# Own buffers for residual loads, spills issued by ScalarE, score banks for the cross output, and two activation sums moved beside cross attention, in a hybrid encoder step on one core

## The chip, the cores and the metric

The kernel runs on one core of a Trainium2 chip. A time is the device time of one execution in microseconds (us). The kernel before takes 1830.3 us, the median of 3 runs (1829.97 to 1832.38). One more execution was profiled; all rows below come from it. It took 1833.62 us, of which 1831.8 us lie between its first and its last instruction (the span).

The engines are named as in the profile: PE multiplies matrices, PEld loads its weights, DVE, ACT and POOL work elementwise, SP issues transfers (DMA). Each engine takes its instructions in order, so an instruction that waits holds back all that stand behind it on its engine. That holds for issues of transfers too: a transfer that is not yet allowed to start holds back the next ones of the same engine.

## The reference

One layer of a streaming encoder, on 1024 prompt frames and 32 sample frames of width 1024, in float32:

```python
z = rms_norm(x, g_mix) @ w_in            # q k v conv_h conv_B conv_C gate_a gate_b
a = window_attention(q, k, v) @ w_attn_out
bo = (cb * causal_conv3(cc * ch)) @ w_conv_out
x = x + (sigmoid(ga) * a + sigmoid(gb) * bo) @ w_mix_out
hc = rms_norm(x, g_cross)                # 4 heads x 64 against 256 memory tokens
x = x + softmax((hc @ w_cq) @ mem_k.T / 8) @ mem_v @ w_co
hm = rms_norm(x, g_mlp)
x = x + square(relu(hm @ w_up)) @ w_down # hidden width 4096
y = rms_norm(x, g_final)
```

It also returns new keys, values, convolution rows and memory keys and values.

## The kernel before

**Layout.** Activations lie transposed, features on the 128 partitions, frames along the free axis. The 1056 frames are cut into three chunks, 0, 1 and 2, of 384, 384 and 288 frames; 1024 features are eight blocks, numbered by f or k. Every float32 number is split in a high part (a rounded copy, made by ACT) and a low part (the rest, a subtraction on DVE), and a product is three matmuls: high by high, low by high, high by low (`gemm`, lines 166 to 168). A gemm over eight blocks is 24 matmuls.

**Weights.** A weight tile of 128x1024 is loaded by SP into `wr` (2 buffers), cast by ACT to `wh` (line 114, or 140 where the low part is fetched) and subtracted by DVE to `wl` (line 115), 3 buffers each. `next_w` keeps up to three weights prepared ahead of the gemm that uses them. Some weights are used for every chunk; for every second of them (`kept`) the low part is written to DRAM when it is first made (`wl_d`, line 145) and read back later (line 139).

**Stages.** After input projection, window attention, convolution and gates come, chunk by chunk, `trunk(c)` (eight items `do_conv_out`, eight items `do_mix`), and cross attention `cross_steps(c)`: statistics, two query products (`do_cq`), per head `scores`, `turn` (transpose of the softmax) and `values`, then two items `do_co` and statistics. `beside` interleaves them: one step of `cross_steps(c)` after each item of `trunk(c+1)`, so that PE has a gemm while DVE and ACT do the softmax. The steps of chunk 2 stand beside the first quarter of the MLP's up product, `up0(0)` and `up0(1)`. `normed_split` (lines 923 to 929) makes the MLP's input for chunks 0 and 1: DVE makes `ct`, SP writes it to DRAM as `xn_d`, ACT and DVE split it.

**Up product.** The other three quarters of the up product for chunks 0 and 1 use a 2x2 product with fewer multiplications. It needs sums of activation blocks: T2, N1, N3, N4 for each k of 0 to 3. `combine(k)` (lines 958 to 973) reads four blocks of `xn_d` into `lt` and makes all four sums and their parts; it runs beside the up products of chunk 2 (`do_up(j, 2)`). POOL also adds pairs of weights there (`s`, lines 992 to 995).

**Buffers.** Temporaries of all kinds share six buffers `ct` (`tmp`), the loads of `m1_d` in `do_conv_out` and of the input `x` in `do_mix` too. PE's results go to PSUM: three buffers `acc`, two banks for the scores `sc` (tag `s`), two `pt`, one `o`. `do_co` puts its four results per item into `acc`.

**Order.** Instructions are ordered per engine by a scheduler that works with a model of times when the program is built; `pin` keeps some in program order. The order is then fixed.

Of the kernel before, what the change touches and what calls it, by code (L numbers as in the profile page):

```python
# [10 lines left out]
F32 = mybir.dt.float32  # L11
F32R = mybir.dt.float32r
AF = mybir.ActivationFunctionType
ALU = mybir.AluOpType
# [4 lines left out]
P = 128  # L19
# [4 lines left out]
NF = 8  # L24
# [14 lines left out]
def hybrid_step(ctx: ExitStack, tc: tile.TileContext, io):  # L39
    nc = tc.nc  # L40
    act, dve, pool_e, pe, sp = nc.scalar, nc.vector, nc.gpsimd, nc.tensor, nc.sync
# [3 lines left out]
    def nm(s):  # L45
        uid[0] += 1
        return f"{s}_{uid[0]}"
# [14 lines left out]
    ps = ctx.enter_context(tc.tile_pool(name="ps", bufs=1, space=PSUM))  # L62
# [16 lines left out]
    xn_d = [dram.tile([P, NF, n], F32, name=f"xn_d{c}") for c, (_, n) in enumerate(CH[:2])]  # L79
# [4 lines left out]
    def pin(ins):  # L84
        return tc.keep_in_program_order(ins)

    def acc_tile(shape):
        return ps.tile(shape, F32, tag="acc", bufs=3, name=nm("acc"))

    def tmp(n, dt=F32):  # L90
        return tp.tile([P, n], dt, tag="ct", bufs=NCT, name=nm("ct"))
# [9 lines left out]
    plan, worder, kept = [], [], {}  # L101
# [29 lines left out]
    def issue_w():  # L131
        if not fetched:
            fetch_w()
        raw = fetched.pop(0)
        key = worder[wpos[0]]
        hi = wp.tile([P, 1024], F32R, tag="wh", name=nm("wh"))
        lo = wp.tile([P, 1024], F32R, tag="wl", name=nm("wl"))
        if kept.get(key) is not None:
            sp.dma_start(lo.bitcast(F32), kept[key])
            act.copy(hi, raw)  # L140
        else:
            split(hi, lo, raw)
            if key in kept:
                kept[key] = dram.tile([P, 1024], F32, name=nm("wl_d"))
                sp.dma_start(kept[key], lo.bitcast(F32))
        ready.append((worder[wpos[0]], (hi, lo)))
        wpos[0] += 1

# [494 lines left out]
    for i, h in enumerate(hosts):  # L643
# [9 lines left out]
        if h[0] == "Q":  # L653
            fn, key = do_Q(h[1], h[2], extras), qt(h[1], h[2])
        elif h[0] == "K":
            fn, key = do_K(h[1], extras), ("w_in", 8 + h[1])
        elif h[0] == "G":
            fn, key = do_gate(h[1], extras), ("w_in", 34 + h[1])
# [71 lines left out]
    def gain_split(x, g, c):  # L730
        hi, lo = yslot(c), yslot(c)
        scaled_split(hi, lo, x, g)
        return hi, lo

    def do_conv_out(c, f):
        def fn(w):
            n = CH[c][1]
            t1 = tmp(n)
            sp.dma_start(t1, m1_d[c][:, f])
            a = acc_tile([P, n])  # L740
            gemm(a, w, bcp[c])
            t = tmp(n)
            dve.tensor_mul(t, a, sg[c][f])  # L743
            (dve if f == NF - 1 else pool_e).tensor_tensor(t, t, t1, op=ALU.add)  # L744
            mg[c][f] = (mslot(n), mslot(n))
            split(*mg[c][f], t)

        return fn

    def do_mix(c, f):  # L750
        def fn(w):
            n = CH[c][1]
            xt = tmp(n)
            sp.dma_start(xt, io[f"x{c}"][:, f])
            a = acc_tile([P, n])
            gemm(a, w, mg[c])
            x = gate_slot(c, f)
            dve.tensor_add(x, a, xt)  # L758
            x1[c][f] = x
            xc[c][f] = gain_split(x, G_CROSS + f, c)  # L760
            square_acc(x, f, c, on_pool=f < NF - 1)

        return fn
# [30 lines left out]
    qc, co = {}, [[None, None] for _ in CH]  # L794
# [91 lines left out]
    def do_co(c, half):  # L886
        def fn(w):
            n = CH[c][1]
            wh, wl = w
            fs = range(4 * half, 4 * half + 4)  # L890
            for f in fs:
                a = acc_tile([P, n])
                for k in range(2):
                    s = slice(((f % 4) * 2 + k) * P, ((f % 4) * 2 + k) * P + P)
                    hi, lo = co[c][k]
                    pe.matmul(a, wh[:, s], hi, start=(k == 0), stop=False)
                    pe.matmul(a, wh[:, s], lo, start=False, stop=False)
                    pe.matmul(a, wl[:, s], hi, start=False, stop=(k == 1))
                x = x1[c][f]
                dve.tensor_add(x, a, x)  # L900
                if half == 0 and c == 2:
                    xm[c][f] = gain_split(x, G_MLP + f, c)
                square_acc(x, f, c)
            if half == 1 and c == 2:
                for f in fs:
                    xm[c][f] = gain_split(x1[c][f], G_MLP + f, c)

        return fn
# [11 lines left out]
    def lt(n=384):  # L920
        return L["pool"].tile([P, n], F32, tag="lt", bufs=6, name=nm("lt"))

    def normed_split(c, f):
        t = tmp(CH[c][1])
        pin(dve.scalar_tensor_tensor(t, x1[c][f], col(G_MLP + f), R[c], op0=ALU.mult, op1=ALU.mult))
        sp.dma_start(xn_d[c][:, f], t)
        hi, lo = xm[c][f] = (yslot(c), yslot(c))
        act.copy(hi, t)
        pin(dve.tensor_sub(lo, t, hi.bitcast(F32)))

    def hidden(c, j, h):
# [21 lines left out]
    def comb_slot(kind, k):  # L953
        if kind in ("N1", "N3"):
            return mslot(384)
        return L["pool"].tile([P, 384], F32R, tag="hx", bufs=8, name=nm("hx")) if k < 2 else yslot(1)

    def combine(k):
        b12, b22, b11, b21 = (lt() for _ in range(4))
        for t, c, f in ((b12, 1, k), (b22, 1, k + 4), (b11, 0, k), (b21, 0, k + 4)):  # L960
            sp.dma_start(t, xn_d[c][:, f])
        n3, n1, t2, n4 = b22, b12, b11, b21
        pin(dve.tensor_sub(n3, b12, b22))
        pin(dve.tensor_sub(n1, b11, b12))
        pin(dve.tensor_sub(t2, b11, n3))
        pin(pool_e.tensor_tensor(n4, b21, t2, op=ALU.subtract))
        for kind, x in (("T2", t2), ("N1", n1), ("N3", n3), ("N4", n4)):
            hi, lo = comb[kind, k] = (comb_slot(kind, k), comb_slot(kind, k))
            act.copy(hi, x)
            if kind[0] == "T" or kind == "N1":  # L970
                pin(dve.tensor_sub(lo, x, hi.bitcast(F32)))
            else:
                pin(pool_e.tensor_tensor(lo, x, hi.bitcast(F32), op=ALU.subtract))

# [174 lines left out]
    def beside(steps, fillers, late=()):  # L1151
        for i, filler in enumerate(fillers):
            item(*filler)
            for x in [x for at, x in late if at == i]:
                item(lambda x=x: x())
            if steps:
                kind, what = steps.pop(0)
                for x in what:
                    if kind == "items":
                        item(*x)  # L1160
                    else:
                        item(lambda x=x: x())
        return steps
# [9 lines left out]
    left = beside([], trunk(0))  # L1173
    left = beside(cross_steps(0), trunk(1))

    normed = lambda c, at: [(at + f, lambda f=f: normed_split(c, f)) for f in range(NF)]
    left = beside(left + cross_steps(1), trunk(2), normed(0, 6))
    left = beside(left + cross_steps(2), up0(0) + up0(1), normed(1, 0))
    assert not left
    for j in range(NF):  # L1180
        item(*do_up(j, 2))
# [223 lines left out]
```

## Time and profile before

| | us | note |
|---|---|---|
| median of 3 runs | 1830.3 | 1829.97 to 1832.38 |
| profiled execution | 1833.62 | |
| its span | 1831.8 | mean granted clock of PE 0.993 |
| PE busy | 1797.5 | 98% |
| DVE busy | 1045.2 | 57% |
| ACT busy | 720.3 | 39% |
| POOL busy | 356.4 | 19% |

The table gives busy time in the whole span. Trunk and cross attention lie at about 800 to 1165 us, the up products of chunk 2 with `combine` at about 1165 to 1210 us. In rows that show instructions, the columns are start, duration, engine, line, operation, result<-operands, and in brackets the idle time of the engine before it with the instruction that ended it. A row of stretches gives the stretch, its length, the busy time of PE, PEld, DVE, ACT and POOL with their instruction counts, the clock that PE was granted (1.00 is full), the share of DMA time, and GB/s. A row of waits gives the total, the number and the longest.

### The profile page before, as it was taken

How to read it: one execution, taken by the hardware profiler on the slowest of the kernel's cores; microseconds unless marked ns; L12 is line 12 of the kernel's file. 1: busy time of each engine (PE TensorE's matmuls, PEld its weight loads, DVE VectorE, ACT ScalarE, POOL GpSimd, SP SyncE). 2: the span in 40 equal slices, each digit the busy share in tenths (PEclk: the TensorE clock that was granted, in tenths of full speed). 3: DMA queues.
4: the chain of work that ended last, by engine and by line, in shares of the span. 5: the costliest groups of instructions: out<-in, count | busy, mean ns of one | idle time of the engine just before them, and what ended most of it. 6: DMA issues, size and time to landing. Idle time of an engine off the chain costs nothing.

```text
span 1831.8 us, 29560 instructions
## 1 busy us (share of the span) xinstructions
PE 1797.5 (98%) x11364; PEld 1780.0 (97%) x11364; DVE 1045.2 (57%) x2007; ACT 720.3 (39%) x1414; POOL 356.4 (19%) x381
## 2 busy tenths in 40 slices
PE   7999999999999999999999899999999999999997
PEld 7999999999999999999999899999999999999997
DVE  7766766757664222436575877766555664242255
ACT  7643535434354101324555655532222443030134
POOL 3211010211100000004333231564433000000023
PEclk9999999999999999999999999999999999999999
DMA  5411111112123124227656666833322664131144
GB/s 177 141 62 62 62 56 60 67 60 71 56 82 119 55 94 134 96 77 244 243 180 227 221 214 217 289 119 103 108 95 88 217 222 149 50 113 42 67 146 145
DMA packets 112205, 230.40 MB, mean 126 GB/s; under 512 B 13344, under 2 KB 74944, under 8 KB 111936
## 3 DMA queue, kind: packets, MB, share of 16 engines
q1 hardware_dynamic: 112064, 228.51, 37.1%
q8 instruction: 90, 1.47, 0.3%
q14 instruction: 51, 0.42, 0.1%
HBM read 181.98 MB, written 46.48 MB: 125 GB/s over the span
## 4 chain that ended last, share of the span: by engine, by line
PE 91%; DVE 3%; DMA 2%; POOL 1%; issue 1%; ACT 1%; SPq 0%; POOLq 0%; DVEq 0%; ACTq 0%
PE acc L166 23%; PE acc L167 23%; PE acc L168 23%; PE acc L1010 3%; PE acc L1012 3%; PE acc L1011 3%; PE pt L535 1%; PE pa L167 1%; PE pa L168 1%; PE pa L166 1%; DVE wl L115 1%; PE sc L510 1%; PE sc L509 1%; DMA ct<-in_x 1%; PE o L548 1%
## 5 line engine op out<-in xcount | busy, mean ns | idle before, releaser
L114 ACT CAST wh<-wr 128x1024 fp32r<-128x1024 f32 x200 | 210.0, 1050 | 486.9 <-PE acc L167 387.4
L166 PE MATMUL acc<-X,wh 128*128 128x384 f32 (+1 forms) x1200 | 390.5, 325 | 8.4 <-ACT wh L114 7.9
L167 PE MATMUL acc<-X,wh 128*128 128x384 f32 (+1 forms) x1200 | 387.8, 323 | 2.0 <-DVE X L241 1.9
L168 PE MATMUL acc<-X,wl 128*128 128x384 f32 (+1 forms) x1200 | 386.8, 322 | 0.3 <-DVE wl L115 0.3
L166 PE MATMUL acc<-Y,wh 128*128 128x384 f32 (+1 forms) x1008 | 326.5, 324 | 1.3 <-DVE ct L940 0.6
L168 PE MATMUL acc<-Y,wl 128*128 128x384 f32 (+1 forms) x1008 | 326.0, 323 | 0.0
L167 PE MATMUL acc<-Y,wh 128*128 128x384 f32 (+1 forms) x1008 | 325.7, 323 | 0.0
L115 DVE TENSOR_TENSOR wl<-wr,wh 128x1024 fp32r<-128x1024 f32 x200 | 267.4, 1337 | 72.9 <-ACT wh L114 72.2
L166 PEld LDWEIGHTS acc<-X,wh 128*128 128x128 f32 x1200 | 226.3, 189 | 9.1 <-ACT wh L114 7.9
L167 PEld LDWEIGHTS acc<-X,wh 128*128 128x128 f32 x1200 | 226.6, 189 | 3.5 <-DVE X L241 3.0
L168 PEld LDWEIGHTS acc<-X,wl 128*128 128x128 f32 x1200 | 226.2, 189 | 0.8 <-DVE wl L115 0.8
L166 PEld LDWEIGHTS acc<-Y,wh 128*128 128x128 f32 x1008 | 189.1, 188 | 2.3 <-DVE ct L940 0.8
L167 PEld LDWEIGHTS acc<-Y,wh 128*128 128x128 f32 x1008 | 189.2, 188 | 0.0
L168 PEld LDWEIGHTS acc<-Y,wl 128*128 128x128 f32 x1008 | 189.1, 188 | 0.0
L237 POOL TENSOR_TENSOR xacc<-xacc,ct 128x384 f32<-128x384 f32 (+1 forms) x62 | 78.3, 1265 | 356.8 <-ACT ct L235 352.0
L166 PE MATMUL acc<-M,wh 128*128 128x384 f32 (+1 forms) x320 | 104.9, 329 | 0.3 <-DVE Ga L758 0.3
L167 PE MATMUL acc<-M,wh 128*128 128x384 f32 (+1 forms) x320 | 104.3, 327 | 0.0
L168 PE MATMUL acc<-M,wl 128*128 128x384 f32 (+1 forms) x320 | 104.3, 326 | 0.0
L114 ACT CAST PTh<-pt 128x512 fp32r<-128x512 f32 (+3 forms) x94 | 46.3, 516 | 129.6 <-PE pt L535 122.4
L744 POOL TENSOR_TENSOR ct<-ct,ct 128x384 f32<-128x384 f32 (+1 forms) x21 | 25.5, 1214 | 364.7 <-DVE ct L743 329.5
L1121 DVE TENSOR_TENSOR Gb<-acc,Gb 128x384 f32<-128x384 f32 (+1 forms) x60 | 31.4, 523 | 110.7 <-PE acc L168 110.7
L166 PE MATMUL acc<-H,wh 128*128 128x288 f32 (+1 forms) x256 | 80.7, 315 | 0.0
(283 smaller groups left out, 3483.7 us busy)
## 6 DMA issues: line engine op xcount, KB each, us to landing
wr<-in_w_down SPq DMA_DIRECT2D x56, 512.0 KB, 3.3
wr<-in_w_in SPq DMA_DIRECT2D x50, 512.0 KB, 3.2
wr<-in_w_up SPq DMA_DIRECT2D x48, 512.0 KB, 3.8
wl<-wl_d SPq DMA_DIRECT2D x28, 512.0 KB, 4.5
wr<-in_w_conv_out SPq DMA_DIRECT2D x24, 512.0 KB, 4.3
wr<-in_w_mix SPq DMA_DIRECT2D x24, 512.0 KB, 4.0
ct<-hid_d SPq DMA_DIRECT2D x64, 192.0 KB, 3.6
hid_d<-lt SPq DMA_DIRECT2D x48, 192.0 KB, 1.8
```

The lines of the kernel that those rows point to most:

```text
L114: act.copy(hi, src)
L115: dve.tensor_sub(lo, src, hi.bitcast(F32))
L166: pe.matmul(out, wh[:, a], hi, start=(k == 0), stop=False)
L167: pe.matmul(out, wh[:, a], lo, start=False, stop=False)
L168: pe.matmul(out, wl[:, a], hi, start=False, stop=(k == len(acts) - 1))
L237: pool_e.tensor_tensor(acc, acc, sq, op=ALU.add)
L509: pe.matmul(sc[:, h, j * w : j * w + w], q[h], a, start=True, stop=False)
L744: (dve if f == NF - 1 else pool_e).tensor_tensor(t, t, t1, op=ALU.add)
L1010: pe.matmul(acc, wh[:, a], hi, start=(start and k == 0), stop=False, skip_group_check=True)
L1011: pe.matmul(acc, wh[:, a], lo, start=False, stop=False, skip_group_check=True)
L1012: pe.matmul(acc, wl[:, a], hi, start=False, stop=(k == 3), skip_group_check=True)
L1121: dve.tensor_add(x, a, x)
```

## The change

Five edits. (1) `ld(n)`: four buffers of its own, in the pool of cross attention, for the loads in `do_conv_out` and `do_mix`. (2) The 14 writes of `wl_d` and the 16 writes of `xn_d` are issued by ACT in place of SP. (3) `do_co` puts the first two of its four results into the two banks of the scores. (4) `combine_n(k)` makes N3 and N1 from three loads into `ld`, after items 4, 6, 8 and 9 of the up product beside cross attention of chunk 2; `combine(k)` keeps T2 and N4, and makes N3 once more without splitting it, since T2 needs it. (5) `normed_split` takes the blocks in the order 0, 4, 1, 5, 2, 6, 3, 7.

```diff
-                sp.dma_start(kept[key], lo.bitcast(F32))
+                act.dma_start(kept[key], lo.bitcast(F32))
...
+    def ld(n):
+        return cr.tile([P, n], F32, tag="ld", bufs=4, name=nm("ld"))
...
-            t1 = tmp(n)
+            t1 = ld(n)
             sp.dma_start(t1, m1_d[c][:, f])
...
-            xt = tmp(n)
+            xt = ld(n)
             sp.dma_start(xt, io[f"x{c}"][:, f])
...
+            two = ps.tile([P, 2, 512], F32, tag="s", name=nm("co"))
             for f in fs:
-                a = acc_tile([P, n])
+                a = two[:, f % 4, :n] if f % 4 < 2 else acc_tile([P, n])
...
-        sp.dma_start(xn_d[c][:, f], t)
         hi, lo = xm[c][f] = (yslot(c), yslot(c))
         act.copy(hi, t)
+        act.dma_start(xn_d[c][:, f], t)
...
+    def two_parts(kind, k, x, engine):
+        hi, lo = comb[kind, k] = (comb_slot(kind, k), comb_slot(kind, k))
+        act.copy(hi, x)
+        pin(engine.tensor_tensor(lo, x, hi.bitcast(F32), op=ALU.subtract))
+
+    def combine_n(k):
+        b12, b22, b11 = (ld(384) for _ in range(3))
+        for t, c, f in ((b12, 1, k), (b22, 1, k + 4), (b11, 0, k)):
+            sp.dma_start(t, xn_d[c][:, f])
+        pin(dve.tensor_sub(b22, b12, b22))
+        pin(dve.tensor_sub(b11, b11, b12))
+        two_parts("N3", k, b22, dve)
+        two_parts("N1", k, b11, pool_e)
+
     def combine(k):
         b12, b22, b11, b21 = (lt() for _ in range(4))
...
-        n3, n1, t2, n4 = b22, b12, b11, b21
-        pin(dve.tensor_sub(n3, b12, b22))
-        pin(dve.tensor_sub(n1, b11, b12))
-        pin(dve.tensor_sub(t2, b11, n3))
-        pin(pool_e.tensor_tensor(n4, b21, t2, op=ALU.subtract))
-        for kind, x in (("T2", t2), ("N1", n1), ("N3", n3), ("N4", n4)):
-            hi, lo = comb[kind, k] = (comb_slot(kind, k), comb_slot(kind, k))
-            act.copy(hi, x)
-            if kind[0] == "T" or kind == "N1":
-                pin(dve.tensor_sub(lo, x, hi.bitcast(F32)))
-            else:
-                pin(pool_e.tensor_tensor(lo, x, hi.bitcast(F32), op=ALU.subtract))
+        pin(dve.tensor_sub(b22, b12, b22))
+        pin(dve.tensor_sub(b11, b11, b22))
+        two_parts("T2", k, b11, dve)
+        pin(pool_e.tensor_tensor(b21, b21, b11, op=ALU.subtract))
+        two_parts("N4", k, b21, pool_e)
...
-    normed = lambda c, at: [(at + f, lambda f=f: normed_split(c, f)) for f in range(NF)]
+    normed = lambda c, at: [(at + i, lambda f=f: normed_split(c, f)) for i, f in enumerate((0, 4, 1, 5, 2, 6, 3, 7))]
...
-    left = beside(left + cross_steps(2), up0(0) + up0(1), normed(1, 0))
+    left = beside(left + cross_steps(2), up0(0) + up0(1), normed(1, 0) + [(4, lambda: combine_n(0)), (6, lambda: combine_n(1)), (8, lambda: combine_n(2)), (9, lambda: combine_n(3))])
```

What moves, in three places. First SP, at the mix items of chunk 2 (`trunk(2)` beside cross attention of chunk 1); `ct<-in_x` and `ld<-in_x` are the loads of the last four blocks of x, `xn_d` the writes of chunk 0's MLP input, `wr` and `wl` weights. Before:

```order
L754 DMA ct_11252<-in_x 128x288
L926 DMA xn_d_86<-ct_11213 128x384
L754 DMA ct_11313<-in_x 128x288
L926 DMA xn_d_86<-ct_11288 128x384
L139 DMA wl_11408<-wl_d_9182 128x1024
L128 DMA wr_11497<-in_w_up 128x1024
L926 DMA xn_d_86<-ct_11349 128x384
L754 DMA ct_11411<-in_x 128x288
L128 DMA wr_11570<-in_w_up 128x1024
L754 DMA ct_11505<-in_x 128x288
```

And now:

```order
L757 DMA ld_11250<-in_x 128x288
L757 DMA ld_11311<-in_x 128x288
L128 DMA wr_11244<-in_w_co 128x1024
L139 DMA wl_11172<-wl_d_9096 128x1024
L757 DMA ld_11408<-in_x 128x288
L128 DMA wr_11305<-in_w_mix 128x1024
L757 DMA ld_11501<-in_x 128x288
L128 DMA wr_11354<-in_w_co 128x1024
```

The same four loads (11252, 11313, 11411, 11505 before; 11250, 11311, 11408, 11501 now) stood behind writes of `xn_d` and behind the first loads of `w_up`; now no write stands between them, and the last of them comes ahead of the second tile of `w_co`.

Second PE, at the first `do_co` of chunk 1. `Y_1922` and `Y_1923` (now `Y_1920`, `Y_1921`) are the attended heads 0 and 1, `Y_1924` and `Y_1925` heads 2 and 3, `o` the last head's values, `M` the mix gemm beside it. Before, the first `do_co` item begins, the values of the last head being one whole mix gemm back:

```order
L168 MATMUL acc_11315<-M_10918,wl_11174 128x288
L896 MATMUL acc_11362<-Y_1922_10948,wh_11248 128x384
L897 MATMUL acc_11362<-Y_1923_10949,wh_11248 128x384
L898 MATMUL acc_11362<-Y_1922_10948,wl_11249 128x384
L896 MATMUL acc_11362<-Y_1924_10950,wh_11248 128x384
L897 MATMUL acc_11362<-Y_1925_10951,wh_11248 128x384
L898 MATMUL acc_11362<-Y_1924_10950,wl_11249 128x384
L896 MATMUL acc_11372<-Y_1922_10948,wh_11248 128x384
```

And now:

```order
L901 MATMUL co_11360<-Y_1920_10946,wh_11246 128x384
L902 MATMUL co_11360<-Y_1921_10947,wh_11246 128x384
L903 MATMUL co_11360<-Y_1920_10946,wl_11247 128x384
L901 MATMUL acc_11380<-Y_1920_10946,wh_11246 128x384
L902 MATMUL acc_11380<-Y_1921_10947,wh_11246 128x384
L903 MATMUL acc_11380<-Y_1920_10946,wl_11247 128x384
L872 MATMUL o_11293<-PTh_11232,mv_9374 128x384
L872 MATMUL o_11293<-PTl_11233,mv_9374 128x384
L872 MATMUL o_11293<-PTh_11240,mv_9379 128x384
L872 MATMUL o_11293<-PTl_11241,mv_9379 128x384
L901 MATMUL acc_11391<-Y_1920_10946,wh_11246 128x384
L902 MATMUL acc_11391<-Y_1921_10947,wh_11246 128x384
```

The half that needs only heads 0 and 1 is done for three results, two of them ahead of the last head's values; a whole mix gemm of 24 matmuls follows (result 11410), and the half with heads 2 and 3 comes after that.

Third POOL, at the up products of chunk 2. `lt<-lt,lt` is N4, `M<-lt,M` the low part of N3, `Y<-lt,Y` that of N4, `ct<-ct` the square of the hidden layer, `s` the sums of weights. Before:

```order
L966 TENSOR_TENSOR lt_12911<-lt_12911,lt_12910 128x384
L944 TENSOR_TENSOR ct_13149<-ct_13147 128x288
L973 TENSOR_TENSOR M_12929<-lt_12909,M_12928 128x384
L973 TENSOR_TENSOR Y_2415_12933<-lt_12911,Y_2414_12932 128x384
L944 TENSOR_TENSOR ct_13220<-ct_13218 128x288
L966 TENSOR_TENSOR lt_12975<-lt_12975,lt_12974 128x384
L973 TENSOR_TENSOR M_12993<-lt_12973,M_12992 128x384
L973 TENSOR_TENSOR Y_2433_12997<-lt_12975,Y_2432_12996 128x384
```

And now:

```order
L986 TENSOR_TENSOR lt_12951<-lt_12951,lt_12950 128x384
L949 TENSOR_TENSOR ct_13055<-ct_13053 128x288
L966 TENSOR_TENSOR Y_2425_12964<-lt_12951,Y_2424_12963 128x384
L1007 TENSOR_TENSOR s_2469_13175<-wr_13094,s_2468_13174 128x512
L1009 TENSOR_TENSOR s_2468_13174<-wr_13094,wr_2453_13095 128x512
L986 TENSOR_TENSOR lt_13006<-lt_13006,lt_13005 128x384
```

The four low parts into `M` are gone from this place; four (now of N1) stand earlier, between the squares of `up0(1)`.

## The prediction

> **What bounds the kernel now.** I read the page's first and fourth parts first, the engines' busy time and the chain of work that ended last.
>
> ```profile
> span 1831.8 us, 29560 instructions
> PE 1797.5 (98%) x11364; PEld 1780.0 (97%) x11364; DVE 1045.2 (57%) x2007; ACT 720.3 (39%) x1414; POOL 356.4 (19%) x381
> PE 91%; DVE 3%; DMA 2%; POOL 1%; issue 1%; ACT 1%; SPq 0%; POOLq 0%; DVEq 0%; ACTq 0%
> ```
>
> PE is the bound: 34.3 us of the span are all that it idles, so no edit off PE can return more than that, and what PE loses to a lower clock. The next question is where. I cut the region that the diff touches into stretches of 10 us; these are the ones that lose most to idle time or a low clock (columns: stretch, length, PE, PEld, DVE, ACT, POOL, clock, DMA share, GB/s).
>
> ```profile
> 1030.00:1040.00 10.00, 7.99 (x56) 7.30 (x56) 8.00 (x14) 6.93 (x12) 2.18 (x3) 1.00 0.72 243
> 1040.00:1050.00 10.00, 7.06 (x34) 5.60 (x34) 7.74 (x13) 5.21 (x10) 4.46 (x4) 0.79 0.73 241
> 1050.00:1060.00 10.00, 9.09 (x44) 8.07 (x44) 6.67 (x11) 4.97 (x9) 5.51 (x6) 0.70 0.36 114
> 1140.00:1150.00 10.00, 8.82 (x57) 8.08 (x57) 6.17 (x13) 4.75 (x13) 1.49 (x2) 1.00 0.62 200
> 1170.00:1180.00 10.00, 9.39 (x71) 9.15 (x70) 8.10 (x12) 5.30 (x8) 5.16 (x6) 1.00 0.76 281
> 1180.00:1190.00 10.00, 9.21 (x69) 8.98 (x69) 8.17 (x10) 4.05 (x6) 9.51 (x8) 1.00 0.83 272
> 1190.00:1200.00 10.00, 9.03 (x62) 8.79 (x61) 9.17 (x10) 4.43 (x7) 9.51 (x8) 1.00 0.67 214
> 1210.00:1220.00 10.00, 8.23 (x38) 7.91 (x37) 2.34 (x3) 1.95 (x2) 5.03 (x6) 0.83 0.32 102
> sum 360.00, PE 347.35 PEld 339.48 DVE 247.97 ACT 191.08 POOL 137.33; mean PE 9.65 PEld 9.43 DVE 6.89 ACT 5.31 POOL 3.81
> ```
>
> From 900 to 1260 PE idles 360 - 347.35 = 12.65 us. The clock rows add (0.21 + 0.30 + 0.17) x 10 = 6.8 us in which slow matmuls count as busy. So 19.5 us is the most that the change can return; the other 21.6 us of idle time lie outside, where it changes nothing. Over half of the 19.5 lies in one place, 1030 to 1060: 2.01 + 2.94 + 0.91 idle and 5.1 of clock, 11.0 us. That is the end of cross attention of chunk 1 beside `trunk(2)`. The timeline of PE there:
>
> ```profile
> 1038.90 0.44 PE L869 MATMUL o<-PTh,mv 128*128 128x384 f32 x1 [1.68 <-DVE tO L872]
> 1044.61 0.44 PE L896 MATMUL acc<-Y,wh 128*128 128x384 f32 x1 [1.46 <-DVE Gb L758]
> 1044.89 0.33 PE L897 MATMUL acc<-Y,wh 128*128 128x384 f32 x1
> 1045.06 0.34 PE L898 MATMUL acc<-Y,wl 128*128 128x384 f32 x1
> 1045.80 0.69 PE L896 MATMUL acc<-Y,wh 128*128 128x384 f32 x1 [0.40 <-ACT Y L878]
> 1046.92 0.69 PE L897 MATMUL acc<-Y,wh 128*128 128x384 f32 x1 [0.43 <-DVE Y L884]
> 1052.23 0.52 PE L898 MATMUL acc<-Y,wl 128*128 128x384 f32 x1
> 1052.55 0.52 PE L896 MATMUL acc<-Y,wh 128*128 128x384 f32 x1
> ```
>
> Two kinds of wait: for a PSUM buffer that DVE has not emptied (L872, L758), and for the last heads (L878, L884). The third and fourth row start 0.17 us apart, at the full clock, the last two 0.32, at the low one. Why is DVE late? It waits in order for x:
>
> ```profile
> 1033.28 0.46 DVE L758 TENSOR_TENSOR Ga<-acc,ct 128x288 f32<-128x288 f32 x1 [1.94 <-DMA ct<-in_x]
> 1050.91 0.46 DVE L758 TENSOR_TENSOR Gb<-acc,ct 128x288 f32<-128x288 f32 x1 [1.82 <-DMA ct<-in_x]
> L758 DVE TENSOR_TENSOR Gb<-acc,ct 128x384 f32<-128x384 f32 x10 | 5.5, 554 | 17.3 <-DMA ct<-in_x 15.7 <-PE acc L168 1.6
> 1036.81 0.33 SPq L926 DMA_DIRECT2D xn_d<-ct  x1
> 1038.32 0.42 SPq L754 DMA_DIRECT2D ct<-in_x  x1
> ```
>
> The two rows of SP are issues. Its waits from 900 to 1260, in total, number and longest:
>
> ```profile
> SPq L926 <- DVE ct L925: 23.9, 10, 4.7
> ```
>
> DVE waits for x, x is issued late by SP, and SP waits for DVE to make `ct` before it may write `xn_d`: a loop through SP's order. Edits 1 and 2 cut it at both ends.
>
> **The change part by part.** *Loads into `ld`, `xn_d` from ACT, `co` in the score banks (1030 to 1060, 11.0 us).* Removed: the waits for x and those of DVE's lag. The new order puts half of `do_co` ahead of the last head's values and a mix gemm of 24 matmuls between the halves, which covers the 0.40 and 0.43. What stays: part of the 1.68, since there is still one `o` buffer and DVE is 80% busy there; I keep half (0.8), and for the first products' own latencies the sum of the two small waits (0.8) and as much again for lost clock, 2.4 in all. Gain 8.6; ends 4 (only the 1.94 + 1.82 of DVE come back) and 11.0.
>
> The 1.2 us at 1140 to 1150 are the wait for the last head in chunk 2, where the new order also has a whole gemm between the halves; I take 1.0, ends 0 and 1.2. A score bank that holds a result is free again after one add on DVE; two further results and a mix gemm lie between that and its next use, so this new wait costs nothing, and without that cover one add, 0.55 us (the mean of the L758 row), per item.
>
> The Trainium skill, TensorE: Matmul & The Clock Gate, Part 1, lets the clock fall only after an idle window of about 3.4 us. The trace differs: no wait above is longer than 1.68 us, and the clock fell. By the row, the clock comes back when the short gaps go; by the rule, it need not.
>
> *N1 and N3 moved out of 1170 to 1220 (4.1 us idle, 1.7 of clock, 5.8 in all).* POOL is 95% busy there. These are the prices and the wait that ends last:
>
> ```profile
> L973 POOL TENSOR_TENSOR M<-lt,M 128x384 fp32r<-128x384 f32 x4 | 5.3, 1330 | 0.0
> L971 DVE TENSOR_TENSOR M<-lt,M 128x384 fp32r<-128x384 f32 x4 | 5.5, 1366 | 0.0
> L964 DVE TENSOR_TENSOR lt<-lt,lt 128x384 f32<-128x384 f32 x4 | 3.9, 964 | 2.1 <-DMA lt<-xn_d 2.1
> L963 DVE TENSOR_TENSOR lt<-lt,lt 128x384 f32<-128x384 f32 x4 | 2.7, 669 | 0.6 <-DMA lt<-xn_d 0.6
> L969 ACT CAST M<-lt 128x384 fp32r<-128x384 f32 x8 | 4.1, 511 | 7.6 <-DVE lt L964 7.6
> 1215.38 0.44 PE L1010 MATMUL acc<-hx,wh 128*128 128x384 f32 x1 [1.77 <-ACT wh L114]
> ```
>
> POOL loses four instructions, 5.3 us; DVE 5.5 + 3.9 = 9.4; ACT 4.1. The wait of 1.77 is for weights whose sums POOL makes last, so 5.3 us less on POOL clears it, and part of the clock loss (1.7) with it. The other waits there hang on loads of `xn_d` and `w_up` that stay. I take 3.0; ends 0 and 5.8.
>
> *What that work costs where it goes (1090 to 1165).* N3 is made twice now, so DVE gets there 4 x (0.67 + 0.96 + 1.37) = 12.0 us, POOL 5.3, ACT 4.1, SP twelve loads of 192 KB. The first row is the room in a stretch of 50 us, the two others are what an evacuation that is a little late costs PE there today:
>
> ```profile
> 1100.00:1150.00 50.00, 48.82 (x309) 48.06 (x308) 35.88 (x74) 28.72 (x71) 8.82 (x10) 1.00 0.65 218
> 1088.52 0.44 PE L166 MATMUL acc<-Y,wh 128*128 128x384 f32 x1 [0.45 <-DVE ct L942]
> 1093.39 0.44 PE L166 MATMUL acc<-Y,wh 128*128 128x384 f32 x1 [0.28 <-DVE ct L802]
> ```
>
> DVE has 14 us free in 50, and 12 are asked for. If each of the twelve DVE instructions delays an evacuation by about 0.25 us that reaches PE, near the smaller row, it costs 3.0 us; ends 0 (all in gaps) and 10 (most of the 12.0 on the path).
>
> *Thirty issues on ACT.* At 0.33 us each (the `xn_d` row above) 9.9 us, where ACT is busy 28.72 of 50 us (the row above): nothing, as PE's weights are cast two gemms ahead. The 16 of `xn_d` stand behind a cast that already needed `ct`, so they wait for nothing. (No ACT issue is in the trace; the ends are 0 and 0.42 us each, the L754 issue above, 12.6 in all, off PE's path.) The 14 of `wl_d` wait for DVE's `wl`, with the next casts behind them; that is the third rival. The order of blocks 0, 4, 1, 5 only lets N3's loads begin earlier: nothing by itself. Those loads wait on SP until ACT's write has landed, with loads of `w_up` behind them; that lies within the 10 above.
>
> The Trainium skill, DMA: Bandwidth & Descriptors, "Issuing engines are not separate DMA queues", says that issuing from another engine saves only issue time, small beside the transfer. By that rule edit 2 returns nothing. What the trace prices is not issue time but the 23.9 us for which SP stood in front of writes.
>
> Sum: 8.6 + 1.0 + 3.0 - 3.0 = 9.6 us. The profiled execution, 1833.6 us (the span and 1.8 around it), would go to 1824.0. It lies 3.3 above the median of the runs, so the median goes from 1830.3 to 1820.7. The likeliest case's own range: with 6 to 11 in place of 8.6 and 1 to 5 in place of the last 3.0, 1816 to 1825.
>
> **The rivals.** *The moved sums cost what they save.* DVE has 2 us to spare where they go, and it is slower where POOL is busy (a 128x384 operation takes 0.55 us in the L758 row, and 1.37 in the L971 row, from where POOL is 95% busy); four more POOL instructions come with them. For: DVE is the engine PE waits for there. Against: the idle 4.1 us at 1170 are as real. Then 3.0 gained meets 8 lost: 9.6 - 5 = 4.6, 1825.7 us.
>
> *The clock does not come back.* At 1040 to 1060 some gap is left after all, and the matmuls there keep the low clock. For: gaps of 0.40 and 0.43 us stand at the start of its fall. Against: before 1040 the clock stood at 1.00 in spite of the 1.68. Then 5.1 of the 8.6 is missing: 4.5 gained, 1825.8 us. The rule of the Trainium skill named above (TensorE: Matmul & The Clock Gate, Part 1) would lead here too, since by it the short gaps did not cause the low clock.
>
> *ACT takes SP's place (slower).* SP's waits in front of `wl_d` and of weights were:
>
> ```profile
> SPq L145 <- DVE wl L115: 34.8, 11, 11.2
> SPq L128 <- DVE wl L115: 80.1, 28, 5.7
> L115 DVE TENSOR_TENSOR wl<-wr,wh 128x1024 fp32r<-128x1024 f32 x62 | 86.6, 1396 | 19.2 <-ACT wh L114 18.9
> L114 ACT CAST wh<-wr 128x1024 fp32r<-128x1024 f32 x63 | 66.0, 1048 | 62.7 <-PE acc L167 26.8 <-DMA wr<-in_w_up 9.5 <-issue 7.9
> ```
>
> The first row is 3.2 us on average, 11.2 at most. ACT now stands in that wait, and casts of weights, exponentials and head copies stand behind it. Two gemms of 24 matmuls at 0.17 us are 8.2 us of lead, less 1.05 for the cast and 1.40 for the low part: 5.8 us. From a hold of 5.8 us on, PE waits; a hold of 11.2 costs 5.4 and about as much clock again as at 1040 (2.5). Two such holds, 15.8, outweigh the 9.6: 1836.5 us. Against it: in the new order most of these issues stand one to three instructions behind their own cast, so a hold should be about one `wl`, 1.4 us.
>
> *It does not do what it says.* SP still stands 80.1 us in front of weights (second row), and a load into `ld` behind a weight that waits is as late as before; a fifth load also waits until the first `ld` is read, with weights behind it. Against: in the new order no write stands between the loads. Then 4 of the 8.6 return, and the sums, whose loads go through the same queue, gain nothing: 9.6 - 4.6 - 3.0 = 2.0, 1828.3 us.
>
> **How the numbers follow.** The forecast 0.50; moved sums cost what they save 0.14; clock 0.09; ACT 0.15; no effect 0.12. A measurement tells 0.2%, 3.7 us, from no change: faster is below 1826.6, slower above 1834.0. Faster: all 0.50 of the forecast, 0.12 of the moved sums, 0.07 of the clock (both cases lie just under 1826.6) and 0.02 of no effect, 0.71; slower: 0.13 of ACT's 0.15; same: the rest, 0.16. The time is that of the forecast, 1820.7. The range runs from the sum of the gains' upper ends, 11.0 + 1.2 + 5.8 = 18.0 us, at 1812, to 1832; it leaves out ACT's case and a little more.
>
> **What would show it.** Right: in the rows of idle time before DVE's L758 the load of x is gone; from 1030 to 1060 the clock is at 1.00 and PE idles under 2 us; SP has no wait in front of `xn_d`; from 1170 to 1220 PE idles under 2.5 us; PE idles 3 us more than now between 1090 and 1165. Wrong: PE waits for casts of `wh` with ACT held in front of `wl_d`; a clock below 0.9 in any stretch from 1030 to 1165; a new wait for a score bank held by `co`; or PE's idle time unchanged with the waits merely under other names.

## The result, and the profile after

| | median us | lowest to highest | runs |
|---|---|---|---|
| before | 1832.38 | 1829.97 to 1836.21 | 5 |
| after | 1844.86 | 1843.17 to 1847.11 | 5 |

The ratio is 1.0068 (95% interval 1.0052 to 1.0085): the change makes the kernel slower by 12.5 us, where 9.6 us less were forecast. The profiled execution took 1845.38 us. Its span and its engines' busy time:

```profile
span 1843.6 us, 29554 instructions
PE 1802.2 (98%) x11364; PEld 1785.2 (97%) x11364; DVE 1048.8 (57%) x2011; ACT 720.6 (39%) x1414; POOL 363.1 (20%) x381
```

The span is 11.8 us longer. PE is still the bound and does the same 11364 matmuls, but it idles 41.4 us of the span instead of 34.3 and takes 4.7 us longer for the matmuls. Here are the stretches of 10 us that answer to those of the prediction, and the worst new ones, in the same columns (the sum is over 900 to 1260):

```profile
980.00:990.00 10.00, 7.51 (x58) 7.28 (x56) 3.37 (x9) 5.98 (x10) 3.72 (x4) 1.00 0.72 253
990.00:1000.00 10.00, 9.68 (x40) 9.69 (x41) 6.27 (x19) 4.19 (x10) 2.39 (x3) 0.66 0.49 181
1030.00:1040.00 10.00, 10.00 (x78) 9.96 (x76) 9.05 (x18) 8.72 (x19) 5.31 (x5) 1.00 0.82 273
1040.00:1050.00 10.00, 8.35 (x58) 7.67 (x56) 10.00 (x18) 7.15 (x13) 4.17 (x3) 1.00 0.76 251
1050.00:1060.00 10.00, 8.53 (x54) 8.24 (x55) 9.33 (x17) 6.00 (x11) 5.43 (x5) 1.00 0.67 232
1170.00:1180.00 10.00, 9.49 (x61) 9.21 (x59) 5.56 (x11) 5.57 (x10) 2.72 (x3) 0.83 0.42 139
1180.00:1190.00 10.00, 5.20 (x21) 4.81 (x21) 5.78 (x12) 2.47 (x4) 4.10 (x5) 0.73 0.88 282
sum 360.00, PE 340.62 PEld 334.47 DVE 242.72 ACT 184.84 POOL 142.66; mean PE 9.46 PEld 9.29 DVE 6.74 ACT 5.13 POOL 3.96
```

The place that the forecast aimed at did come back: from 1030 to 1060 PE loses 1.65 + 1.47 = 3.1 us in place of 11.0, at the full clock. Yet idle time over 900 to 1260 rose from 12.65 to 360 - 340.62 = 19.38. The loss moved to three other places. The same three stretches in both kernels, before first:

```profile
970.00:1000.00 30.00, 29.69 (x194) 29.21 (x195) 16.86 (x39) 17.32 (x30) 11.05 (x10) 1.00 0.63 214
1060.00:1100.00 40.00, 39.13 (x244) 38.15 (x243) 29.02 (x55) 20.55 (x37) 14.40 (x13) 1.00 0.69 230
1150.00:1200.00 50.00, 47.63 (x331) 46.68 (x330) 39.49 (x56) 27.29 (x46) 35.08 (x30) 1.00 0.79 276
```

And after:

```profile
970.00:1000.00 30.00, 27.20 (x161) 26.96 (x160) 15.85 (x35) 16.34 (x30) 13.86 (x13) 0.89 0.59 214
1060.00:1100.00 40.00, 36.44 (x219) 35.54 (x219) 25.70 (x48) 19.76 (x37) 15.28 (x13) 0.96 0.58 197
1150.00:1200.00 50.00, 42.36 (x259) 40.49 (x259) 31.29 (x51) 24.32 (x44) 24.95 (x23) 0.90 0.81 269
```

Idle time there goes from 3.55 to 14.00 us, and the clock, 1.00 before, costs 0.11 x 30 + 0.04 x 40 + 0.10 x 50 = 9.9 us: 20.4 us lost, against 7.9 gained at 1030 to 1060. What PE waits for in them, from its timeline after (`pq` is the sum of squares over the partitions, `pr` the broadcast of the scale worked out from it):

```profile
985.76 0.72 PE L191 MATMUL pq<-ones,xacc 128*128 128x1 f32 x6
990.32 0.69 PE L209 MATMUL pr<-ct,ones_r 128*128 128x384 f32 x1 [2.80 <-ACT ct L207]
1077.00 0.72 PE L191 MATMUL pq<-ones,xacc 128*128 128x1 f32 x6
1080.30 0.44 PE L209 MATMUL pr<-ct,ones_r 128*128 128x384 f32 x1 [1.94 <-ACT ct L207]
1179.77 0.40 PE L209 MATMUL pr<-ct,ones_r 128*128 128x288 f32 x1 [0.51 <-ACT ct L207]
1180.91 0.40 PE L210 MATMUL pr<-ct,ones_r 128*128 128x288 f32 x1 [0.73 <-DVE ct L208]
1185.38 0.61 PE L166 MATMUL acc<-Y,wh 128*128 128x288 f32 x1 [4.07 <-DVE ct L945]
```

Each chunk has a wait for the same thing, the statistics of x after cross attention. The last row, 4.07 us, comes after the broadcast. ACT copies the broadcast to `R`, and DVE needs `R` to empty the first buffer of the up product. In ACT's order this copy (L220) stands behind the cast of a weight of `w_up` whose load is late:

```profile
1183.29 1.05 ACT L140 CAST wh<-wr 128x1024 fp32r<-128x1024 f32 x1 [3.57 <-DMA wr<-in_w_up]
1184.36 0.40 ACT L220 COPY R<-pr 128x288 f32<-128x288 f32 x1
```

The broadcast had ended at 1181.31 (1180.91 + 0.40), so some 3 of the 4.07 us are this order on ACT and the late load. Before, the statistics of chunk 0 were not waited for at all:

```profile
979.58 0.72 PE L191 MATMUL pq<-ones,xacc 128*128 128x1 f32 x6
985.70 0.34 PE L209 MATMUL pr<-ct,ones_r 128*128 128x384 f32 x1
```

Why are the statistics late? The sum needs all eight blocks of x. DVE adds the cross output to them, four blocks for each `do_co`. The last three adds of chunk 0, before:

```profile
972.12 1.48 DVE L900 TENSOR_TENSOR Gb<-acc,Gb 128x384 f32<-128x384 f32 x3
```

and adds out of `co` after:

```profile
968.49 0.56 DVE L905 TENSOR_TENSOR Ga<-co,Ga 128x384 f32<-128x384 f32 x1 [2.31 <-PE co L903]
972.14 0.56 DVE L905 TENSOR_TENSOR Gb<-co,Gb 128x384 f32<-128x384 f32 x1
977.43 0.56 DVE L905 TENSOR_TENSOR Gb<-co,Gb 128x384 f32<-128x384 f32 x1 [3.41 <-PE co L903]
```

The two late adds, each after an idle wait of DVE, are those of the second result in the `co` tile. The last add ends at 978.0 instead of 973.6; ACT's square and POOL's sums follow it.

### The profile page after: what moved, and what is told of

Same layout as the page of the kernel before. It is cut to its first block, busy times and chain, and to the rows that moved or that the text cites. A ratio compares the mean times of both kernels' runs of the same rounds, so it can differ in the third digit from the quotient of the medians.

```text
span 1843.6 us, 29554 instructions
## 1 busy us (share of the span) xinstructions
PE 1802.2 (98%) x11364; PEld 1785.2 (97%) x11364; DVE 1048.8 (57%) x2011; ACT 720.6 (39%) x1414; POOL 363.1 (20%) x381
## 3 DMA queue, kind: packets, MB, share of 16 engines
q8 instruction: 90, 1.47, 0.3%
## 4 chain that ended last, share of the span: by engine, by line
PE 89%; DVE 4%; DMA 3%; ACT 2%; issue 2%; SPq 0%; POOL 0%; POOLq 0%; DVEq 0%; ACTq 0%
PE acc L166 22%; PE acc L167 22%; PE acc L168 22%; PE acc L1024 3%; PE acc L1025 3%; PE acc L1026 3%; PE pt L535 1%; PE pa L168 1%; PE pa L167 1%; PE pa L166 1%; DVE wl L115 1%; PE sc L510 1%; PE sc L509 1%; PE o L548 1%; PE o L547 1%
## 5 line engine op out<-in xcount | busy, mean ns | idle before, releaser
L166 PE MATMUL acc<-Y,wh 128*128 128x384 f32 (+1 forms) x1008 | 330.2, 328 | 7.6 <-DVE ct L945 4.1
L167 PE MATMUL acc<-Y,wh 128*128 128x384 f32 (+1 forms) x1008 | 329.2, 327 | 0.0
L166 PEld LDWEIGHTS acc<-Y,wh 128*128 128x128 f32 x1008 | 192.6, 191 | 9.0 <-DVE ct L945 4.3
L167 PEld LDWEIGHTS acc<-Y,wh 128*128 128x128 f32 x1008 | 192.4, 191 | 0.0
L237 POOL TENSOR_TENSOR xacc<-xacc,ct 128x384 f32<-128x384 f32 (+1 forms) x62 | 82.2, 1329 | 358.0 <-ACT ct L235 355.5
L747 POOL TENSOR_TENSOR ct<-ct,ld 128x384 f32<-128x384 f32 (+1 forms) x21 | 23.8, 1138 | 372.0 <-DVE ct L746 344.4
```

What stands on the lines that cost most here:

```text
L166: pe.matmul(out, wh[:, a], hi, start=(k == 0), stop=False)
L167: pe.matmul(out, wh[:, a], lo, start=False, stop=False)
L237: pool_e.tensor_tensor(acc, acc, sq, op=ALU.add)
```

## The experiments

T1, formed from this: `co` is one tile of two banks, and the program keeps order by tiles. The matmuls of the second result wait for DVE's add of the first, in another bank. So the program's order puts other matmuls between them, the last block of x comes late, and PE reaches the broadcast before the statistics are there. R1: the moved sums are the cost. R2: ACT held in front of its DMA issues is the cost (the cast above waits for a load, not for an issue).

**Parts of the change.** First the change without edit 3:

```diff
-            two = ps.tile([P, 2, 512], F32, tag="s", name=nm("co"))
-                a = two[:, f % 4, :n] if f % 4 < 2 else acc_tile([P, n])
+                a = acc_tile([P, n])
```

> The changed kernel with edit 3 undone: all four results of do_co in acc buffers again. Theory T1 (the two results that share the one tile of the score banks wait for DVE's add of the first, the last blocks of x come some 4 us later, and with them the sums of squares, for which PE then stands): the 10 us that 800 to 1270 lost more are gone, and what edits 1 and 2 gained stays, so 1822 to 1828 us. R1 (the sums moved into cross attention of chunk 2 are the cost) and R2 (ACT held in front of its DMA issues is the cost): stays within 3 us of the change, 1842 to 1848.

Measured: 1833.84 us, ratio to before 1.0006 (0.9996 to 1.0015). The 11 us are gone, as T1 says, and R1 and R2 fall as the main cause. But it is not under 1828: the gain looked for from edits 1 and 2 is missing.

Then the kernel before with edit 3 alone (the same lines, added).

> The kernel before with edit 3 alone. T1: some 10 us slower than before, 1839 to 1846, with DVE waiting 2 to 3 us in front of the add for PE's do_co and PE standing over 2 us in front of the broadcast of the statistics. R1 and R2: within 3 us of before, or faster, since only the wait for an acc buffer is taken away: 1828 to 1834.

Measured: 1842.27 us, 1.0053 (1.0038 to 1.0068). Edit 3 alone makes most of the loss. PE's longest waits from 800 to 1270, in total, number and longest:

```profile
PE pr L209 <- ACT ct L207: 4.0, 2, 2.9
PE acc L166 <- DVE ct L941: 3.7, 1, 3.7
```

The kernel before with edits 1 and 2 alone (`ld` in place of `tmp` for both loads, `wl_d` and `xn_d` written by ACT):

> The kernel before with edits 1 and 2 alone (own load buffers, writes issued by ACT). T1: the gain that was forecast from 1030 to 1060 without the price, 1822 to 1829, clock there at 1.00. R2: slower than before by most of 12 us, 1838 to 1846. R1: as T1.

Measured: 1832.56 us, 1.0001 (0.9991 to 1.0011): neither the gain nor the loss, and the clock was not at 1.00 as T1 had it (0.88 from 1040 to 1050, 0.78 from 1050 to 1060). DVE's evacuation of the mix gemms, whose idle time was put down to the load of x (before, the first row; with edits 1 and 2, the second; both 900 to 1260):

```profile
L758 DVE TENSOR_TENSOR Gb<-acc,ct 128x384 f32<-128x384 f32 (+1 forms) x10 | 5.0, 502 | 14.2 <-DMA ct<-in_x 12.6 <-PE acc L168 1.6
```

```profile
L761 DVE TENSOR_TENSOR Gb<-acc,ld 128x384 f32<-128x384 f32 (+1 forms) x10 | 5.0, 502 | 12.1 <-PE acc L168 12.1
```

The load is on time, and DVE still stands 12.1 of the 14.2 us, now for PE. And PE's timeline with edits 1 and 2 alone:

```profile
1048.32 1.33 PE L899 MATMUL acc<-Y,wh 128*128 128x384 f32 x3 [1.66 <-ACT Y L881]
1051.17 0.69 PE L900 MATMUL acc<-Y,wh 128*128 128x384 f32 x1 [1.52 <-DVE Y L887]
```

PE's wait for the last head, 0.40 and 0.43 before, has grown to 1.66 and 1.52. The waits for x and for the head lay one behind the other, and most of what one gave back the other took: from 1030 to 1060 PE lost 8.6 us here, 11.0 before.

The kernel before with edits 4 and 5 alone (the moved sums and the order of blocks):

> The kernel before with edits 4 and 5 alone (combine_n beside cross attention of chunk 2, blocks in the order 0, 4, 1, 5). T1: within 4 us of before, 1828 to 1836. R1: slower by most of 12 us, 1838 to 1846, with PE's new idle time between 1090 and 1190. R2: within 3 us of before.

Measured: 1835.63 us, 1.0014 (1.0005 to 1.0024): 3.4 us by the medians, a small part of the loss. Both sides of the forecast's terms can be read here: first the stretch to which the work went, before and with the moved sums, then the one that it left, with the moved sums:

```profile
1090.00:1165.00 75.00, 73.53 (x461) 72.22 (x460) 57.69 (x107) 46.07 (x100) 22.37 (x22) 1.00 0.71 245
1090.00:1165.00 75.00, 70.36 (x422) 68.29 (x421) 61.00 (x113) 45.19 (x103) 26.24 (x24) 0.98 0.78 262
1170.00:1220.00 50.00, 48.43 (x335) 47.74 (x335) 27.25 (x41) 17.26 (x27) 32.77 (x28) 1.00 0.63 211
```

In the first, idle time and lost clock go from 1.5 to 4.6 + 1.5 us, so 4.7 are lost (3.0 forecast). In the other they go from the 5.8 of the prediction to 1.6, so 4.2 are gained (3.0 forecast).

**What in edit 3 costs.** The same banks, with both products ahead of the two adds:

```diff
+                for g in {0: (), 1: (f - 1, f)}.get(f % 4, (f,)):
-                x = x1[c][f]
-                dve.tensor_add(x, a, x)
+                    x = x1[c][g]
+                    dve.tensor_add(x, two[:, g % 4, :n] if g % 4 < 2 else a, x)
...
-                square_acc(x, f, c)
+                    square_acc(x, g, c)
```

> The kernel before with edit 3, but both results in the score banks are made before the two adds that read them, so that no result waits for the add of its neighbour; the same banks are held, and the last product of do_co keeps its place among PE's instructions. T1: the price of edit 3 is gone, at most 3 us from before on the slow side, 1826 to 1835, and no wait of over 1 us for the statistics from 980 to 990 and from 1160 to 1190. Rival T1b (the scores' banks being held, or DVE's adds being late, is the price, not the order of the two results): as slow as edit 3 alone, 1839 to 1846.

Measured: 1827.82 us, 0.9976 (0.9966 to 0.9986), 14.5 us below edit 3 alone, and faster than before. T1b falls: the banks are held no shorter. Edit 3's order of instructions on PE, with what each row waits for (`DVE_49` is the semaphore by which DVE reports its progress; rows 5883 to 5902 go on with the mix gemm):

```
5876 L898 MATMUL co_10218<-Y_1664_9847,wh_10116 128x384 [waits DVE_49]
...
5882 L166 MATMUL acc_10268<-M_9340,wh_10170 128x384 [waits DVE_49]
...
5903 L897 MATMUL co_10218<-Y_1661_9844,wh_10116 128x384 [waits DVE_49]
```

And with the adds later:

```
5876 L898 MATMUL co_10218<-Y_1664_9847,wh_10116 128x384 [waits DVE_49]
...
5878 L897 MATMUL co_10218<-Y_1661_9844,wh_10116 128x384
```

The second result follows the first at once and waits for nothing; with an add between them it comes behind 21 of the 24 matmuls of a mix gemm.

Two other ways to have no neighbour in the tile: one bank for the first result alone, or two tiles of one bank each, in the transposes' banks.

```diff
-            two = ps.tile([P, 2, 512], F32, tag="s", name=nm("co"))
+            two = ps.tile([P, 1, 512], F32, tag="s", name=nm("co"))
-                a = two[:, f % 4, :n] if f % 4 < 2 else acc_tile([P, n])
+                a = two[:, 0, :n] if f % 4 == 0 else acc_tile([P, n])
```

> The kernel before with edit 3 for the first of four results alone, so that the tile in the scores' banks holds one result and none has to wait for its neighbour. T1: 1825 to 1833, the gain of edit 3 without its price, with PE's losses from 1030 to 1060 down from 11 us. T1b: part of the price stays, 1836 to 1842.

Measured: 1832.41 us, 0.9998 (0.9989 to 1.0007). No price, and no gain to be measured.

```diff
-                a = two[:, f % 4, :n] if f % 4 < 2 else acc_tile([P, n])
+                a = ps.tile([P, n], F32, tag="pt", bufs=2, name=nm("co")) if f % 4 < 2 else acc_tile([P, n])
```

> The kernel before with edit 3, but the two results in two tiles of their own, a bank each (those of the transposes, which are free after the last head), and the scores' banks untouched. T1: 1823 to 1833. T1b: the same, since the scores' banks are not held; so this run tells T1b from T1 only together with the two others.

Measured: 1833.41 us, 1.0004 (0.9993 to 1.0015), just above what T1 allowed. The timeline of PE shows the same wait in chunk 2:

```profile
1163.68 0.72 PE L191 MATMUL pq<-ones,xacc 128*128 128x1 f32 x6
1169.74 0.40 PE L209 MATMUL pr<-ct,ones_r 128*128 128x288 f32 x1 [2.30 <-ACT ct L207]
```

Here no result waits for its neighbour, so T1 was too narrow: what counts first is how many matmuls the program's order leaves between the sum (L191) and the broadcast (L209). Counted in PE's order of instructions:

| kernel, chunk | rows between | PE waits at L209 and L210, then behind them |
|---|---|---|
| before, 0 / 1 / 2 | 41 / 40 / 43 | none / none / none, then 0.61 |
| change, 0 / 1 / 2 | 7 / 3 / 22 | 2.80 / 1.94 / 0.51 + 0.73, then 4.07 |
| edit 3 in chunk 0 alone, 0 | 12 | 2.84 |
| edit 3 in chunk 2 alone, 2 | 18 | 1.04 + 0.75, then 3.36 |
| two tiles, 1 / 2 | 18 / 22 | none, then 0.83 / 2.30 + 0.74, then 1.21 |
| adds later, 0 / 1 / 2 | 43 / 39 / 32 | none / none / none, then 1.20 |

With 32 rows or more PE never stood at the broadcast, with 12 or fewer it always did. From the sum to a broadcast that waited for it it took 4.6 us in chunk 0 of the change (985.76 to 990.32); at 0.17 us a matmul that is 27 of them. In between the count alone does not decide (22 rows: 0.51 in one kernel, 2.30 in the other), since the scale does not always take as long to make: 3.3 us in chunk 1 of the change (1077.00 to 1080.30), 6.1 in chunk 2 with the two tiles. In the last, DVE's part of the scale ended at 1166.78, but ACT's next step (L207) stood behind a cast:

```profile
1167.83 1.04 ACT L114 CAST wh<-wr 128x1024 fp32r<-128x1024 f32 x1 [2.05 <-DMA wr<-in_w_up]
```

The change with one bank:

> The changed kernel with the tile in the scores' banks holding the first result of four alone. T1: some 11 us faster than the change, 1828 to 1835; if the gains of edits 1 to 3 add up, under 1828. T1b: 1838 to 1845.

Measured: 1834.23 us, 1.0012 (0.9998 to 1.0026), as T1 has it without the gains added up.

**Where it costs.** Edit 3 in one chunk at a time, by `if c == 0` or `if c == 2` at the tile:

> The kernel before with edit 3 for chunk 0 alone, as one tile with an add between its two results. The last product of do_co of that chunk stands 27 matmuls later on PE, at 0.17 us each 4.6 us. T1: slower by about the 4.8 us that edit 3 alone lost from 980 to 1000 (3.05 idle, 1.7 of clock), so 1834 to 1840, with PE standing over 2 us for the statistics between 980 and 1000 and nothing new after 1100. If the price were not in the place but in the mere use of the banks, nothing would change here: 1831 to 1834.

Measured: 1834.33 us, 1.0013 (1.0003 to 1.0023): the lower edge. The wait is there,

```profile
989.78 0.54 PE L209 MATMUL pr<-ct,ones_r 128*128 128x384 f32 x1 [2.84 <-ACT ct L207]
```

and with it 2.87 of idle time and 3.4 of clock from 980 to 1000; but only 2.0 us of it stay in the median. Part came back from 1030 to 1060, where this kernel lost 8.8 us in place of 11.0.

> The kernel before with edit 3 for chunk 2 alone. The last product of do_co of that chunk stands 31 matmuls later on PE, 5.3 us. T1: slower by about what edit 3 alone lost more than before from 1160 to 1190, 10.2 less 1.4, 9 us, less what the rest of 1190 to 1260 gives back, so 1836 to 1842, with nothing new between 980 and 1000. Otherwise 1831 to 1834.

Measured: 1840.10 us, 1.0039 (1.0026 to 1.0052): 7.8 us. PE in chunk 2:

```profile
1170.31 0.40 PE L209 MATMUL pr<-ct,ones_r 128*128 128x288 f32 x1 [1.04 <-ACT ct L207]
1175.21 0.61 PE L166 MATMUL acc<-Y,wh 128*128 128x288 f32 x1 [3.36 <-DVE ct L941]
```

2.0 and 7.8 are 9.8 together, and edit 3 in all chunks cost 10.0. In chunk 2 the wait behind the broadcast is the long one: the up products need the scale `R` before DVE can empty their first buffers. Here too ACT's copy to `R` stands behind a cast of `w_up`; it starts at 1174.19, 2.3 us after the broadcast's end. In the kernel with the adds later the copy stands ahead of that cast and starts right behind the broadcast, which ended at 1163.75:

```profile
1163.79 0.40 ACT L220 COPY R<-pr 128x288 f32<-128x288 f32 x1 [0.52 <-PE pr L210]
```

So a part of edit 3's price in chunk 2 is an order on ACT that came with it; no run takes that part by itself. It can come without late statistics: in the change with one bank, 43 rows lie between sum and broadcast, PE does not stand there, and it still waits 2.96 us for the first buffer of the up product.

**The gains together.** Edits 1 and 2, and edit 3 with the later adds:

> Edits 1 and 2, and edit 3 with both products made before the two adds; no moved sums. If the gain that was forecast for 1030 to 1060 needed all three (the loads on time, the banks free), 1822 to 1827, under edit 3 with the later adds alone (1827.8). If edits 1 and 2 return nothing (they gave 1.0001 alone, DVE's wait for x becoming a wait for PE), the same as that one, 1826 to 1831.

Measured: 1826.10 us, 0.9966 (0.9952 to 0.9981); repeated below, 1826.66. Both expected ranges hold it; whether edits 1 and 2 add the last microsecond to 0.9976 isn't resolved. It is faster than both kernels. From 1030 to 1060 PE lost 2.80 us there at the full clock, one wait:

```profile
1044.18 0.37 PE L166 MATMUL acc<-M,wh 128*128 128x288 f32 x1 [2.80 <-DVE Gb L761]
```

The whole change with the later adds:

> The whole change, with both products of edit 3 made before the two adds. T1: 12 to 17 us faster than the change, 1827 to 1833; against the run without the moved sums it shows their price once more, 2 to 4 us by the run of the moved sums alone (1.0014), and 0 by the forecast.

Measured: 1832.39 us, 1.0002 (0.9993 to 1.0011). The order of two adds, with all that the scheduler moves with it, is 12.5 us of the change. But with the moved sums the kernel is 6 us slower than without them, more than the 2 to 4 expected.

**The moved sums.** Open was whether edit 4 or edit 5 is that price. The kernel of 1826.10 once more, then with edit 5, then with edit 4 alone:

> Edits 1 and 2 and edit 3 with the later adds once more, in more rounds, as the base of the two next runs: 0.9966 before (0.9952 to 0.9981), so 1824 to 1829 us.

Measured: 1826.66 us, 0.9971 (0.9960 to 0.9982).

> That kernel with edit 5 alone (blocks in the order 0, 4, 1, 5, 2, 6, 3, 7). If the order costs what the moved sums cost on this base (1832.4 against 1826.1), 1830 to 1834; by the forecast nothing, 1824 to 1829.

Measured: 1827.15 us, 0.9965 (0.9955 to 0.9975): the order of blocks costs nothing by itself.

> That kernel with edit 4 alone (N1 and N3 beside cross attention of chunk 2), blocks in the old order. If the twelve more DVE instructions and the loads are the price, 1829 to 1836, at or above the run with edits 4 and 5; if edit 5 is the price, 1824 to 1828; by the forecast 3.0 gained and 3.0 lost, 1824 to 1829.

Measured: 1836.74 us, 1.0025 (1.0013 to 1.0037), 10 us above its base and 0.7 above the range for this case: edit 4 is the price, and edit 5 takes some 4 us of it back. PE in chunk 2 with edit 4:

```profile
1141.91 0.40 PE L901 MATMUL co<-Y,wh 128*128 128x288 f32 x1 [1.12 <-DVE Y L887]
1149.30 0.41 PE L900 MATMUL co<-Y,wh 128*128 128x288 f32 x1 [1.38 <-ACT Y L881]
1176.79 0.61 PE L166 MATMUL acc<-Y,wh 128*128 128x288 f32 x1 [3.26 <-DVE ct L945]
```

In the base the waits for the last head are not among PE's waits. DVE is held from 1100 to 1150 with edit 4 by what the sums load:

```profile
DVE ld L973 <- DMA ld<-xn_d: 2.7, 3, 1.5
```

So, by these rows, the moved sums stand on DVE and wait for their loads there, and the last heads' work comes behind them. The rows between sum and broadcast fall from 32 to 26, and the wait for the up products' first buffer, 3.26 with edit 4, was 1.20 in the base. With edit 4 the copy to `R` stands behind a cast that waits 2.84 us for its load; in the base it does not. How much of the 10 us is DVE's wait, how much the cover that PE lost and how much ACT's order was not taken apart.

## Why the prediction was wrong

**The failed step** is in the first term, on edit 3: "A score bank that holds a result is free again after one add on DVE; two further results and a mix gemm lie between that and its next use, so this new wait costs nothing, and without that cover one add, 0.55 us [...] per item." The next use was taken to be the next item's. It is the second result of the same item, since the two share a tile. And the price was not an add: it was most of a gemm of delay for the last block of x, and behind it PE at the broadcast. In chunk 2 ACT's copy to `R` behind a late cast came on top. In place of 0 to 0.55 us per item, 3.3 us for all six, it was 12.5 us (1844.86 against 1832.39, with nothing but the order of the adds changed in the program). The order of instructions shown ahead of the prediction had it: result 11360 first, two others, and no second `co` result among those rows.

**The first term's gain, 8.6 us.** At its place it came (11.0 to 3.1 lost, DVE's wait for x gone, full clock). But its parts did not add up as the forecast put them. Edits 1 and 2, said to return at least 4, return nothing that the median shows by themselves. "DVE waits for x" was read as the cause because it ended the idle time of the engine PE waits for; with x on time DVE waits for PE and PE for the last head. Edit 3 with the later adds returns 4.8 us alone, and all three 5.8 to 6.2, against 8.6 + 1.0 for these two terms.

**The moved sums, 3.0 gained and 3.0 lost.** They lose about 6 us net on the base of 1826, 3.4 alone. Alone, both sides showed at their places and within their bounds, 4.2 gained and 4.7 lost. On the base of 1826 the gain was gone: from 1170 to 1220 PE loses 6.0 us in the base and 5.8 with the moved sums, since that stretch now begins with the wait for the scale `R`.

The three together, 12.5 us for edit 3's order, 6 for the moved sums and 3.6 for the smaller gain (9.6 forecast, 6.0 there), are the 22 us between forecast and result.

**The thirty issues on ACT** cost nothing that can be measured together with the own buffers, 1.0001, as forecast; without the buffers they were not run.

**The rivals.** ACT in SP's place gave the nearest time, by a mechanism that is not there: edits 1 and 2 alone contain it and lose nothing. "The moved sums cost what they save" was right in size (its 5 us net against some 6) but not the main cause. The clock did come back at 1040, and was lost at the new waits. "It does not do what it says" holds for the gain of edits 1 and 2, not for its reason: the loads are on time.

**Signs.** Of those named, the load wait of L758 went, and SP no longer stands before `xn_d`; from 1030 to 1060 PE idles 3.1 us, not under 2; from 1170 to 1220 it idles 5.7, not under 2.5; from 1090 to 1165 it idles 0.7 us (75 - 74.27), less than the 1.5 before, where 3 more were forecast. Two of the signs named for a wrong forecast came: a clock below 0.9 (0.83 from 1080 to 1090, 0.66 even earlier), and a new wait on the banks of `co`, though inside the item.

## What to carry to other kernels

Before two results share a tile, ask whether the program orders the second's writes behind the first's reads, and then follow the last of the results to the next thing that needs all of them: the price is not the wait but how much work is left between a reduction and its first use (here the first use could come 3.3 to 6.1 us after the sum). Look, too, at what stands ahead of the reduction's own steps on the other engines: here a cast that waited for its load. A wait seen on an engine off the path is only worth removing if the next wait behind it is shorter; a run with that part alone tells it for the price of one kernel. Work moved into a gap of DVE counts with its loads, because DVE waits for them in order, with the critical heads behind.

## What the runs showed of the hardware that was not expected

The granted clock does not follow the length of the wait. The kernel with edits 1 and 2 and the later adds was profiled twice. At the same place PE stood 2.80 us (the row of 1044.18 above), with the clock at 1.00, as its stretches show,

```profile
1040.00:1050.00 10.00, 7.20 (x47) 6.91 (x46) 9.19 (x16) 5.60 (x10) 5.51 (x5) 1.00 0.72 232
```

and in the repeat 2.19 us, from its timeline,

```profile
1044.12 0.58 PE L166 MATMUL acc<-M,wh 128*128 128x288 f32 x1 [2.19 <-DVE Gb L761]
```

with the clock at 0.83:

```profile
1040.00:1050.00 10.00, 7.81 (x42) 7.51 (x42) 8.27 (x14) 5.45 (x10) 7.32 (x5) 0.83 0.61 208
```

In the change a wait of 2.80 was followed by 0.66. The Trainium skill, TensorE: Matmul & The Clock Gate, Part 1, says that the window in which PE's activity is watched runs freely, so that the slow matmuls at the start of one and the same kernel differ from run to run; the pair above agrees with that in the middle of a kernel. That the clock is low after an idle window of about 3.4 us, as it also says, does not cover 0.83 after a wait of 2.19. So a forecast can price the clock behind a wait of 2 to 3 us only as a chance, here between 0 and 3.4 us (0.34 x 10, from the row of 990 above).
